# RWKV pair scores: copy on ACT and select on GpSimd in place of a masked copy on VectorE, with three DMAs of the inverse issued by GpSimd

## The chip, the cores and the metric

One NeuronCore of a Trainium2 chip runs the kernel. The metric is the device time of one execution in microseconds (us), as the median of several runs. Engines are named as the profile names them: PE is TensorE, PEld its weight loads, DVE is VectorE, ACT is ScalarE, POOL is GpSimd, SP is SyncE. Each takes its instructions strictly in the order in which they stand in its queue, so an instruction that waits holds up everything behind it on the same engine. DMAs are issued by instructions that stand in the queue of SP, ACT or POOL.

## The reference

A trunk of two layers over 256 tokens of width 1024. A layer normalises x, projects it for four mixers (stick-breaking attention, RWKV-7, MoBA, HGRN2), gates and sums their outputs, projects again, and runs a SwiGLU FFN. The change lies in the RWKV-7 mixer, which the reference computes token by token:

```
def step(state, inp):
    r_t, w_t, k_t, v_t, a_t, b_t = inp
    sa = jnp.einsum('bhvk,bhk->bhv', state, a_t)
    state = (state * w_t[:, :, None, :] + sa[..., None] * b_t[:, :, None, :]
             + v_t[..., None] * k_t[:, :, None, :])
    return state, jnp.einsum('bhvk,bhk->bhv', state, r_t)
```

The kernel computes it in two chunks of 128 tokens. For each chunk it needs, for each of 4 heads, two masked 128x128 score matrices of b against a and r (LB), the same of k (LK), and the inverse of a triangular matrix made from LB.

## The kernel before, in words

The kernel keeps x in SBUF, streams all weights from HBM as 128x1024 float32 tiles, and splits each into a high part (a cast on ACT, L128) and a low part (a subtraction on DVE, L129), so that each product is made of three matmuls (`mm3`, recorded at L80 like all matmuls). Four split weights stand in SBUF at a time. Matmul results of projections lie in the PSUM tiles `pa` (3 buffers), those of the RWKV stream in `p1` (2), those of the other three mixers in `p2` and `p3`.

`drive` interleaves two generators ("streams") with projection units: one stream is the RWKV mixer, the other runs the remaining three mixers. Each `yield` names a delay, counted on a running estimate of PE's time, after which the stream gets its next turn. The order in which instructions stand on each engine is then set by a scheduler from the order of the code and its own estimates; it sees the engine of each instruction.

In `rwkv`, for each chunk c, `pair_scores` makes the scores of four heads in two PSUM tiles. Before the change POOL fills the SBUF tile `dst` (128 x 4 x 256, of the pool `b1`) with zeros ahead of time (L536), and DVE copies the scores through the mask `armask` (`copy_predicated`, L542), once for each PSUM tile. `armask` is i<t in its first 128 columns and i<=t in its second. `pair_scores` is called four times per layer: for LB of chunk 0 and 1, then for LK of chunk 0 and 1.

The inverse goes through DRAM to change its layout: `send(c)` writes LB of chunk c to `flat` (L548, two DMAs of 256 KB); L564 reads the 64 diagonal 16x16 blocks back as `xb`, once both have landed; DVE inverts them in three levels (L570 to L594) into `yb`; L599 writes `yb` to `tri`; L602 reads it back as `cb`; L606 spreads it. Before the change all five DMAs stand in ACT's queue.

Around this stand, on ACT: the copies of stick-breaking attention's transposed weights `c<-p` (L938), which PE needs for the product with v; and, in `hgrn_proj`, `use_n` (L810, L811) which with L812 on DVE empties the two `pa` tiles of a projection. The next projection unit (a gate unit) needs the first of these buffers.

Of the kernel before, what the change touches and what calls it, by code (L numbers as in the profile page):

```python
# [15 lines left out]
OP = mybir.AluOpType  # L16
# [30 lines left out]
def trunk(ctx, tc, x, w_t, w_n, w_br, w_out, w_gu, w_dn, par, lora, rows, gains, consts, masks, out):  # L47
    nc = tc.nc
# [8 lines left out]
    def sb(tag, width, dt=F32):  # L57
        return mx.tile([128, width], dt, name=tag, tag=tag, bufs=NB[tag])

    def ps(tag):  # L60
        return psum.tile([128, 512], F32, name=tag, tag=tag, bufs=NB[tag])

    def g2d(t, a):
        return t.rearrange("p (a t) -> p a t", a=a)
# [4 lines left out]
    def over(t, n):  # L69
        return t[:, None, :].to_broadcast([128, n, t.shape[-1]])  # L70
# [3 lines left out]
    def mm(o, l, r, start=True, stop=True):  # L74
        n = 1
        for d in r.shape[1:]:
            n *= d
        m = l.shape[-1]
        pe[0] += max(m / 1.2, n / 2.4) if r.dtype == F32R else max(m / 0.6, n / 0.6)
        nc.tensor.matmul(o, l, r, start=start, stop=stop)  # L80
# [105 lines left out]
    for c in range(2):  # L186
        s = slice(c * 512, (c + 1) * 512)
# [7 lines left out]
    for i in range(20):  # L195
        nc.tensor.matmul(warm[:, 0:256], flat1[:, 0:128], flat1[:, 0:256], start=True, stop=True)
        if i in (8, 12):
            c = (i - 8) // 4
# [15 lines left out]
    yb = one.tile([64, 16, 16], F32, name="yb")  # L214
    armask = mk[:, 0:256]
# [220 lines left out]
    def head_sums(q, tag):  # L436
        p = ps(tag)
        for t in range(2):
            for hp in range(2):
                mm_cols(p[:, t * 4 + hp * 2:t * 4 + hp * 2 + 2], q[:, hp, t * 128:(t + 1) * 128], blk2)  # L440
        return p
# [4 lines left out]
    def hrow(a):  # L446
        return slice((a % 2) * 64, (a % 2) * 64 + 64)
# [17 lines left out]
    def rwkv(m, l, yT):  # L465
# [38 lines left out]
        for hp in range(2):  # L504
            s = pp[:, P_KK + hp:P_KK + hp + 1]
# [3 lines left out]
        p = head_sums(sq, "p1")  # L509
# [8 lines left out]
        p = ps("p1")  # L518
# [14 lines left out]

        def pair_scores(src, dst, c):
            p = [ps("p1"), ps("p1")]
            nc.gpsimd.memset(dst, 0.0)  # L536
            for a in range(4):
                hp = a // 2
                mm(p[a % 2][:, hp * 256:(hp + 1) * 256], src[hrow(a), hp, c * 128:(c + 1) * 128],
                   AR[hrow(a), 2 * hp + c].rearrange("p u t -> p (u t)"))  # L540
            for u in range(2):
                nc.vector.copy_predicated(dst[:, u::2], over(armask, 2), g2d(p[u], 2))  # L542

        flat = dram.tile([8, 128 * 129], F32, name="flat")
        tri = dram.tile([64, 256], F32, name="tri")

        def send(c):
            nc.scalar.dma_start(flat[4 * c:4 * c + 4, 0:128 * 128].rearrange("m (s t) -> s m t", s=128),  # L548
                                LB[c][:, :, 0:128])

        for c in range(2):
            LB.append(g2d(sb("b1", 1024), 4))
            pair_scores(bn, LB[c], c)
            yield 1600
            send(c)
# [10 lines left out]
        for c in range(2):  # L566
            LK.append(g2d(sb("b1", 1024), 4))
            pair_scores(kh, LK[c], c)
            yield 3200
# [26 lines left out]
            product(t4, blk(yb, 0, 0), blk(xb, 0, 1))  # L596
            product(blk(yb, 0, 1), t4, blk(yb, 1, 1))
        yield 4000
        nc.scalar.dma_start(tri.rearrange("p (s t) -> p s t", s=16), yb)  # L599
        yield 2500  # L600
        cb = sb("h1", 256)[:, 0:128].rearrange("p (m t) -> p m t", m=8)
        nc.scalar.dma_start(cb, bass.AP(tensor=tri.tensor, offset=tri.offset, ap=[[16, 128], [2048, 8], [1, 16]]))  # L602
# [16 lines left out]
        for c in range(2):  # L619
            z5 = z[c].rearrange("p a (b u h) -> p a b u h", u=2, h=16)  # L620
            p = ps("p1")
# [4 lines left out]
        for c in range(2):  # L626
            p = ps("p1")
# [12 lines left out]
        p = [ps("p1"), ps("p1")]  # L640
# [6 lines left out]
        p = [ps("p1"), ps("p1")]  # L647
# [11 lines left out]
        for c in range(2):  # L659
            z6.append(g2d(sb("h1", 256), 4))  # L660
            p = ps("p1")
# [4 lines left out]
        for c in range(2):  # L666
            zs.append(g2d(sb("h1", 256), 4))
            p = ps("p1")
# [5 lines left out]
        for c in range(2):  # L674
            p = ps("p1")
# [6 lines left out]
        if l:  # L682
            p = ps("p1")
# [11 lines left out]
        p = ps("p1")  # L695
# [6 lines left out]
        p = ps("p1")  # L702
# [10 lines left out]
        p = head_sums(rx, "p1")  # L713
# [7 lines left out]
        p = ps("p1")  # L721
# [8 lines left out]
        for c in range(2):  # L730
            p = ps("p1")
# [9 lines left out]
            p = ps("p1")  # L741
# [3 lines left out]
            u = sb("h1", 256)  # L745
            nc.scalar.copy(u, p[:, 0:256])
            yield 1000
            if c == 0:
                p = ps("p1")
# [7 lines left out]
                for hp in range(2):  # L757
                    for e in range(2):
                        s = hrow(e)
                        nc.vector.tensor_scalar(st[s, hp, s], p[s, hp * 64:(hp + 1) * 64], fac[s, hp:hp + 1],  # L760
                                                None, op0=OP.mult)
            p = ps("p1")
# [350 lines left out]
    def rwkv_s(m, l, yT):  # L1113
        yield from rwkv(m, l, yT)
# [181 lines left out]
```

## Time and profile before

| | us |
|---|---|
| median of 3 runs | 928.75 |
| lowest, highest | 926.98, 929.4 |
| the profiled execution: time | 930.03 |
| the profiled execution: span | 928.2 |
| PE busy in the span | 910.3 (98%) |
| DVE busy | 651.4 (70%) |
| ACT busy | 475.5 (51%) |
| POOL busy | 83.8 (9%) |

Times in the rows are counted from the start of the span. The two layers lie 452.6 us apart at the place of the change (a wait of PE that ends at 113.89 us in layer 0 ends at 566.43 us in layer 1). The granted clock is a share of TensorE's full 2.4 GHz: 0.50 is its lower level, 1.2 GHz.

### The profile page before, as it was taken

To read this page: it belongs to the slowest core of one execution; us is meant where nothing else is said; L and a number is where in the kernel's file an instruction comes from. 1 tells how busy PE (TensorE), PEld (TensorE's weight loads), DVE (VectorE), ACT (ScalarE), POOL (GpSimd) and SP (SyncE) were. 2 spreads that over 40 slices of the span, in tenths; PEclk is the share of its full clock that TensorE was granted. 3 is DMA by queue.
4 is the path that set the end of the run, shared out by engine and by line. 5 is a ranking of instruction groups with operands and counts; after the bars stand their busy time and mean duration, and the time that the engine had idled before them with its cause. 6 is when DMAs were issued, how large, how long until landed. Compare 5 with 4: busy or idle time off the path is not lost.

```text
span 928.2 us, 14996 instructions
## 1 busy us (share of the span) xinstructions
PE 910.3 (98%) x5902; PEld 761.5 (82%) x5902; DVE 651.4 (70%) x957; ACT 475.5 (51%) x726; POOL 83.8 (9%) x94
## 2 busy tenths in 40 slices
PE   8999899999999999999999998999999999999996
PEld 5999678778888888888889986767787888888885
DVE  5668877786766666677567778768678566666665
ACT  5564385445535545456445645644455345555453
POOL 3001100323000000000000201023130000000000
PEclk9999999999999999999999999999999999999999
DMA  8654454345864556568435444533368356666551
GB/s 302 204 159 137 130 175 136 114 147 166 256 220 134 183 183 184 182 206 272 155 114 161 159 140 127 186 103 115 119 208 264 114 181 204 185 182 201 181 181 46
DMA packets 50424, 158.11 MB, mean 170 GB/s; under 512 B 9393, under 2 KB 11953, under 8 KB 50354
## 3 DMA queue, kind: packets, MB, share of 16 engines
q1 hardware_dynamic: 43632, 155.19, 52.4%
q10 hardware_dynamic: 6722, 1.97, 0.9%
q8 instruction: 46, 0.75, 0.3%
q14 instruction: 24, 0.20, 0.1%
HBM read 154.91 MB, written 2.23 MB: 169 GB/s over the span
## 4 chain that ended last, share of the span: by engine, by line
PE 80%; DVE 10%; DMA 4%; issue 2%; ACT 2%; POOL 0%; SPq 0%; ACTq 0%; POOLq 0%; DVEq 0%
PE pa L80 56%; PE p L80 23%; DVE lo L129 2%; PE p L89 1%; PE pa L89 1%; DMA h<-flat 1%; DMA xr<-in_x_dram 1%; DVE b L542 1%; DMA flat<-b 1%; DVE xy L591 1%; DMA raw<-in_w_n_dram 1%; DMA lora<-in_lora_dram 1%; DMA raw<-in_w_gu_dram 1%; DVE b L867 1%; DVE b L965 1%
## 5 line engine op out<-in xcount | busy, mean ns | idle before, releaser
L129 DVE TENSOR_TENSOR lo<-raw,hi 128x1024 fp32r<-128x1024 f32 x268 | 331.0, 1240 | 153.6 <-ACT hi L128 150.6
L128 ACT CAST hi<-raw 128x1024 fp32r<-128x1024 f32 x268 | 279.2, 1048 | 225.5 <-PE pa L80 107.4
L80 PE MATMUL pa<-h,hi 128*128 128x256 f32 (+1 forms) x1280 | 277.9, 339 | 0.0
L80 PEld LDWEIGHTS pa<-h,hi 128*128 128x128 f32 x1280 | 215.9, 190 | 24.6 <-issue 2.0
L80 PE MATMUL pa<-hi,h 128*128 128x512 f32 x576 | 194.1, 402 | 4.6 <-DVE p L812 4.6
L80 PE MATMUL pa<-h,lo 128*128 128x256 f32 x960 | 179.9, 283 | 0.0
L80 PEld LDWEIGHTS pa<-h,lo 128*128 128x128 f32 x960 | 148.6, 191 | 7.0 <-issue 0.7
L80 PEld LDWEIGHTS pa<-hi,h 128*128 128x128 f32 x576 | 109.0, 189 | 31.5 <-DVE p L812 5.5
L80 PE MATMUL pa<-lo,h 128*128 128x512 f32 x288 | 113.6, 394 | 0.0
L80 PE MATMUL p<-hi,c 128*128 128x512 f32 (+1 forms) x352 | 113.4, 394 | 0.0
L80 PEld LDWEIGHTS p<-hi,c 128*128 128x128 f32 x352 | 66.1, 189 | 15.2 <-DVE c L129 0.6
L80 PE MATMUL p<-lo,c 128*128 128x512 f32 (+1 forms) x176 | 69.2, 393 | 0.0
L80 PEld LDWEIGHTS pa<-lo,h 128*128 128x128 f32 x288 | 54.5, 189 | 9.9
L263 POOL TENSOR_TENSOR rs<-rs,half 128x1 f32<-128x1 f32 x10 | 6.0, 597 | 471.6 <-DVE rs L262 471.6
L80 PE MATMUL pa<-hi,y 128*128 128x512 f32 x128 | 44.0, 399 | 0.1
L80 PE MATMUL p<-hi,b 128*128 128x512 f32 x128 | 41.4, 396 | 0.2 <-DVE b L129 0.2
L80 PEld LDWEIGHTS p<-lo,c 128*128 128x128 f32 x176 | 33.1, 188 | 6.8
L1033 POOL TENSOR_TENSOR p<-p,gt 128x512 f32<-128x512 f32 x16 | 30.9, 1953 | 39.4 <-DVE gt L1031 31.8
L340 DVE TENSOR_TENSOR gt<-gt,pa 128x256 f32<-128x256 f32 x80 | 33.2, 414 | 0.0
L128 ACT CAST c<-xy 128x512 fp32r<-128x512 f32 x20 | 12.4, 620 | 39.2 <-DVE xy L1136 39.2
L339 ACT COPY gt<-pa 128x256 f32<-128x256 f32 x80 | 29.3, 366 | 0.0
L80 PEld LDWEIGHTS pa<-hi,y 128*128 128x128 f32 x128 | 24.0, 188 | 6.3 <-issue 0.7
(276 smaller groups left out, 943.4 us busy)
## 6 DMA issues: line engine op xcount, KB each, us to landing
raw<-in_w_gu_dram SPq DMA_DIRECT2D x88, 512.0 KB, 3.9
raw<-in_w_n_dram SPq DMA_DIRECT2D x80, 512.0 KB, 3.6
raw<-in_w_dn_dram SPq DMA_DIRECT2D x44, 512.0 KB, 3.5
raw<-in_w_t_dram SPq DMA_DIRECT2D x40, 512.0 KB, 3.5
raw<-in_w_br_dram SPq DMA_DIRECT2D x16, 512.0 KB, 4.0
raw<-in_w_out_dram SPq DMA_DIRECT2D x16, 512.0 KB, 4.4
b<-in_gains_dram SPq DMA_DIRECT2D x4, 512.0 KB, 5.5
flat<-b ACTq DMA_DIRECT2D x4, 256.0 KB, 3.2
```

What stands on the lines that cost most here:

```text
L80: nc.tensor.matmul(o, l, r, start=start, stop=stop)
L89: nc.tensor.transpose(o, i, ident)
L128: a = nc.scalar.copy(dst[0], src)
L129: return a, (eng or nc.vector).tensor_tensor(dst[1], src, dst[0], op=OP.subtract)
L263: nc.gpsimd.tensor_tensor(dst, dst, half[:, :dst.shape[-1]], op=OP.pow)
L339: nc.scalar.copy(dst, p[:, 256:512])
L340: nc.vector.tensor_tensor(dst, dst, p[:, 0:256], op=OP.add)
L542: nc.vector.copy_predicated(dst[:, u::2], over(armask, 2), g2d(p[u], 2))
L591: nc.vector.tensor_tensor(pr[:, b, i], l4[:, b, i, None].to_broadcast(bc), r.to_broadcast(bc), op=OP.mult)
L867: nc.vector.tensor_tensor(qv, qv, t4[s, :, :, 0:1].to_broadcast([64, 2, 2 * nb, hb]), op=OP.mult)
L965: nc.vector.tensor_tensor_scan(kb, kb, reset[t][:, ::-1], 1.0, op0=OP.mult, op1=OP.add)
L1033: e.tensor_tensor(mg[f, t], mg[f, t], g, op=OP.add)
```

## The change

`pair_scores` no longer fills `dst` with zeros and no longer copies through the mask. ACT copies the whole of each PSUM tile to `dst`, and then POOL zeroes the masked part with two `affine_select` instructions, each over 4 heads x 128 columns, in place. The two `flat` DMAs and the `tri` DMA are issued by POOL in place of ACT. The two reads back (`xb`, `cb`) stay on ACT.

```diff
         def pair_scores(src, dst, c):
             p = [ps("p1"), ps("p1")]
-            nc.gpsimd.memset(dst, 0.0)
             for a in range(4):
                 hp = a // 2
                 mm(p[a % 2][:, hp * 256:(hp + 1) * 256], src[hrow(a), hp, c * 128:(c + 1) * 128],
                    AR[hrow(a), 2 * hp + c].rearrange("p u t -> p (u t)"))
             for u in range(2):
-                nc.vector.copy_predicated(dst[:, u::2], over(armask, 2), g2d(p[u], 2))
+                nc.scalar.copy(dst[:, u::2], g2d(p[u], 2))
+            for u in range(2):
+                v = dst[:, :, u * 128:(u + 1) * 128]
+                nc.gpsimd.affine_select(v, v, [[0, 4], [1, 128]], OP.is_ge, 0.0, base=u - 1, channel_multiplier=-1)
...
         def send(c):
-            nc.scalar.dma_start(flat[4 * c:4 * c + 4, 0:128 * 128].rearrange("m (s t) -> s m t", s=128),
+            nc.gpsimd.dma_start(flat[4 * c:4 * c + 4, 0:128 * 128].rearrange("m (s t) -> s m t", s=128),
                                 LB[c][:, :, 0:128])
...
         yield 4000
-        nc.scalar.dma_start(tri.rearrange("p (s t) -> p s t", s=16), yb)
+        nc.gpsimd.dma_start(tri.rearrange("p (s t) -> p s t", s=16), yb)
```

Line numbers behind this place are two higher after the change. PE's order is the same in both kernels. The orders of ACT, POOL and DVE differ, in both layers alike.

ACT before, from the last cast ahead of the `flat` DMAs to the copies L938 (`flat` is written from LB, h is `xb`, c the attention weights, p_954 and the like are PSUM tiles):

```order
L960 ACTIVATE b_944<-b_933 128x1024
L961 ACTIVATE b_933<-b_933 128x1024
L128 CAST hi<-raw 128x1024
L548 DMA flat<-b_953 128x4x128
L548 DMA flat<-b_1000 128x4x128
L796 COPY p<-pa 128x512
L128 CAST hi<-raw 128x1024
L564 DMA h_1120<-flat 64x16x16
L128 CAST hi<-raw 128x1024 x2
L938 COPY c_1096<-p_1091 128x512
L938 COPY c_1103<-p_1098 128x512
```

ACT after, the same stretch:

```order
L962 ACTIVATE b_944<-b_933 128x1024
L541 COPY b_953<-p_954 128x2x256
L963 ACTIVATE b_933<-b_933 128x1024
L541 COPY b_953<-p_955 128x2x256
L128 CAST hi<-raw 128x1024
L541 COPY b_1001<-p_1002 128x2x256
L541 COPY b_1001<-p_1003 128x2x256
L128 CAST hi<-raw 128x1024
L798 COPY p<-pa 128x512
L566 DMA h_1122<-flat 64x16x16
L128 CAST hi<-raw 128x1024 x2
L940 COPY c_1098<-p_1093 128x512
```

The two `flat` DMAs are gone from ACT and four score copies have come in; the read of `flat` (L564, now L566) still stands ahead of two casts and the attention copies.

ACT before, at the end of the inverse (tri is written from `yb`, h_1372 is `cb`, p<-pa is `use_n`):

```order
L128 CAST hi<-raw 128x1024 x3
L599 DMA tri<-yb 64x256
L810 COPY p<-pa 128x256
L811 ACTIVATE p<-pa 128x256
L602 DMA h_1372<-tri 128x8x16
L810 COPY p<-pa 128x256
L811 ACTIVATE p<-pa 128x256
```

ACT after, the same stretch:

```order
L128 CAST hi<-raw 128x1024 x2
L604 DMA h_1376<-tri 128x8x16
L812 COPY p<-pa 128x256
L813 ACTIVATE p<-pa 128x256
L812 COPY p<-pa 128x256
L813 ACTIVATE p<-pa 128x256
```

The write of `tri` is gone from ACT, and the read of `tri` has moved from between the two pairs of `use_n` to ahead of both.

POOL after, the whole stretch (before, four `L536 MEMSET` stand here and the two products p<-p,cn):

```order
L969 MEMSET b_933 128x4
L544 AFFINE_SELECT b_953<-b_953 128x4x128 x2
L550 DMA flat<-b_953 128x4x128
L544 AFFINE_SELECT b_1001<-b_1001 128x4x128 x2
L550 DMA flat<-b_1001 128x4x128
L984 TENSOR_TENSOR p<-p,cn 128x512 x2
L544 AFFINE_SELECT b_1124<-b_1124 128x4x128 x2
L544 AFFINE_SELECT b_1181<-b_1181 128x4x128 x2
L601 DMA tri<-yb 64x256
L815 TENSOR_TENSOR p<-p,rws 128x256 x2
```

The selects and the DMAs of LB now alternate on one engine, and the write of `tri` stands behind the selects of LK.

## Rows read from the trace of the kernel before

**Rows 1.** Page, part 1: busy time, share of the span and instructions by engine.

```profile
PE 910.3 (98%) x5902; PEld 761.5 (82%) x5902; DVE 651.4 (70%) x957; ACT 475.5 (51%) x726; POOL 83.8 (9%) x94
```

**Rows 2.** Waits of PE, the longest: us in total, times, longest us.

```profile
PE pa L80 <- DVE p L812: 4.6, 2, 2.3
```

**Rows 3.** Timeline of PE: start us, us, what, idle before; one row per layer.

```profile
113.89 0.50 PE L80 MATMUL pa<-hi,h 128*128 128x512 f32 x1 [2.33 <-DVE p L812]
...
566.43 0.50 PE L80 MATMUL pa<-hi,h 128*128 128x512 f32 x1 [2.30 <-DVE p L812]
```

**Rows 4.** Chain that ended last, layer 0, 83 to 119 us: start us, us, what.

```profile
88.81 3.23 DMA flat<-b
...
92.12 3.92 DMA h<-flat
...
111.49 0.68 DVE yb L594
...
112.19 0.49 ACTq L599
...
112.72 0.07 ACT p L810
```

**Rows 5.** Timeline of ACT, layer 0, 81 to 116 us.

```profile
81.17 1.06 ACT L960 ACTIVATE b<-b 128x1024 f32<-128x1024 f32 x1 [0.54 <-DVE b L929]
82.26 1.06 ACT L961 ACTIVATE b<-b 128x1024 f32<-128x1024 f32 x1
...
89.23 0.59 ACT L796 COPY p<-pa 128x512 f32<-128x512 f32 x1 [4.97 <-DVE b L542]
...
94.79 1.07 ACT L938 COPY c<-p 128x512 f32<-128x512 f32 x2
...
115.33 0.38 ACTq L602 DMA_DIRECT2D h<-tri  x1
```

**Rows 6.** Timeline of PE, layer 0: scores of LB and LK, attention times v.

```profile
84.51 1.89 PE L80 MATMUL p<-b,c 64*128 64x256 f32 x8
...
95.26 1.14 PE L80 MATMUL p<-b,c 64*128 64x256 f32 x8
96.33 1.14 PE L80 MATMUL p<-c,p 128*64 128x128 f32 x16
```

**Rows 7.** Timeline of DVE, layer 0, 100 to 114 us.

```profile
100.47 1.33 DVE L542 COPY_PREDICATED b<-mk,p 128x512 f32<-128x512 uint8 x2
101.70 0.99 DVE L981 TENSOR_TENSOR c<-c,cn 128x512 f32<-128x512 f32 x1
...
103.82 0.68 DVE L981 TENSOR_TENSOR c<-c,cn 128x512 f32<-128x512 f32 x1
...
112.08 1.21 DVE L129 TENSOR_TENSOR lo<-raw,hi 128x1024 fp32r<-128x1024 f32 x1
```

**Rows 8.** Groups of POOL by form: busy us, mean ns of one, idle before.

```profile
L1033 POOL TENSOR_TENSOR p<-p,gt 128x512 f32<-128x512 f32 x16 | 30.9, 1953 | 39.4 <-DVE gt L1031 31.8 <-DVE bs L715 7.6
...
L982 POOL TENSOR_TENSOR p<-p,cn 128x512 f32<-128x512 f32 x4 | 4.3, 1096 | 32.9 <-DVE c L980 32.9
...
L263 POOL TENSOR_TENSOR var<-var,half 128x4 f32<-128x4 f32 x4 | 4.1, 1016 | 28.6 <-DVE var L262 28.6
...
L238 POOL MEMSET reset<- 128x512 f32 x2 | 1.0, 520 | 0.0
```

**Rows 9.** DMA issues: KB each, median us from issue to landing.

```profile
tri<-yb ACTq DMA_DIRECT2D x2, 64.0 KB, 3.1
```

**Rows 10.** Stretches around the wait: busy (x) by engine, PEclk, DMA share, GB/s.

```profile
114.00:116.00 2.00, 2.00 (x7) 1.63 (x8) 1.36 (x4) 0.25 (x1) 0.65 (x1) 0.73 0.88 262
116.00:118.00 2.00, 2.00 (x6) 1.52 (x6) 1.04 (x2) 1.98 (x4) 1.06 (x2) 0.50 0.73 188
118.00:120.00 2.00, 2.00 (x10) 1.61 (x9) 2.00 (x4) 1.99 (x8) 0.57 (x1) 0.92 0.12 23
...
566.00:568.00 2.00, 1.57 (x7) 1.31 (x8) 1.90 (x5) 0.00 (x0) 0.73 (x1) 1.00 0.91 292
```

## The prediction

> **What bounds the kernel now.** I read the page's busy times first. PE is busy 98% of the span [rows 1], its order of instructions is the same after the change, and no matmul is added or removed. So the change can only move the few microseconds in which PE stands still. Next I read who PE waits for: by far the longest entry is the wait for L812, 4.6 us in two waits [rows 2], one in each layer, 2.33 and 2.30 us [rows 3]. Then I followed the chain that ends in the first of these waits backwards [rows 4]. PE wants a `pa` buffer; L812 on DVE empties it, but needs L810 and L811 of ACT; these stand in ACT's queue behind the issue of the `tri` DMA (112.19), which waits for the last step of the inverse on DVE (111.49 + 0.68 = 112.17). The inverse starts when `xb` lands (92.12 + 3.92 = 96.04), and that starts when the second `flat` DMA lands (88.81 + 3.23 = 92.04). So the end of PE's wait, 113.89, is set by a chain that begins with the scores of LB, and the change touches nearly every link. The clock is the last thing to read: behind the wait in layer 0 the granted clock is 0.73, 0.50, 0.92 in three stretches of 2 us, so PE was on its lower level for part of it and lost 2 x (0.27 + 0.50 + 0.08) = 1.7 us; behind the wait in layer 1 it is 1.00 at once [rows 10]. So all that can be won by removing these waits is 4.6 + 1.7 = 6.3 us, 0.7% of the time.
>
> **The change part by part.** I work in layer 0's times; layer 1 has the same waits within 0.03 us [rows 3].
>
> *VectorE loses the masked copies.* Four pairs of L542 per layer go. Two of the pairs lie inside the inverse, one at 100.47 and one eight microseconds later; each holds DVE for 101.70 - 100.47 = 1.23 us until the next instruction starts, say 1.25 [rows 7]. The changed order also puts one weight split more behind the inverse that stood ahead of its last step; a split takes 1.21 us [rows 7], of which neighbours overlap a little: about 1.1. From `xb` to the finished `yb` took 112.17 - 96.04 = 16.1 us; 2 x 1.25 + 1.1 = 3.6 come off, which leaves 12.5 us. This is the gain.
>
> *ACT gets the copies.* A copy of 128x512 from PSUM (L796) takes 0.59 us [rows 5]. The first stands behind L960, the second behind L961, so LB of chunk 0 is copied at 81.17 + 1.06 + 0.59 + 1.06 + 0.59 = 84.5. PE wanted the buffers for the scores of chunk 1 at 84.51 and then took 1.89 us where the eight rows of LK take 1.14 [rows 6], since it waited for L542. That wait of 0.8 us goes, and chunk 1 is copied by 84.5 + 1.1 + 2 x 0.59 = 86.8. Eight copies are 4.7 us of ACT per layer. What hides them: ACT stood idle 4.97 us ahead of L796 [rows 5], in front of the `flat` DMAs that leave it.
>
> *POOL gets the selects.* No `affine_select` is in the trace. Its bounds are the nearest rows of POOL at 128x512: 0.52 us for a fill that reads nothing, 1.10 for a product of two tiles at this very place, 1.95 for a product beside a busy DVE [rows 8]. I take t = 1.1, since a select reads and writes and stands where L982 stands. The fills that go were idle time on POOL, so they give nothing back.
>
> *POOL issues `flat` and `tri`.* No DMA of POOL is in the trace either. I write g for what such a DMA takes more than one of ACT, and let the issue hold up POOL as long. From below it is 0, if it flies like ACT's. From above I take one whole further flight, 3.1 us [rows 9]. I take g = 1.0, since a POOL instruction with almost no data, 128x4, takes 1.02 [rows 8], and the issue is at least such an instruction. The Trainium skill, "DMA: Bandwidth & Descriptors", section "Specifications", states about 1 us to the first byte for a DMA of GpSimd, whose descriptors are written by software, against 0.6 us for one of sync or scalar; by that, an estimate from the page, g would be 0.4 and the sum below +0.7 us per layer in place of +2.5. No row here shows it.
>
> *The sum.* Selects of chunk 0, its DMA's issue, selects of chunk 1, its DMA: the second `flat` lands at 84.5 + 2t + g + 2t + g + 3.23 = 94.1, where it landed at 92.04. `xb` lands at 94.1 + 0.05 + 3.92 = 98.1, `yb` is ready at 98.1 + 12.5 = 110.6, which is 1.6 us earlier than now. `tri` lands at 110.6 + g + 3.1 = 114.7. But the read of `tri`, L604, now stands ahead of both pairs of `use_n`, while before only the short issue of the write stood ahead of the first. So ACT's first copy comes at 114.7 + 0.5 = 115.2, where it came at 112.72 [rows 4]. From that copy to PE's restart it took 113.89 - 112.72 = 1.2 us: PE restarts at 116.4, 2.5 us later than now. In short, the shift per layer is 4t + 3g - 4.9 us. The round trip of `tri` has taken the place of what DVE saved.
>
> *A new wait on the way.* ACT waits at L566 for `flat`, and behind it stand two casts and the attention copies L940. Before, L938 was done 94.79 + 1.07 - 92.04 = 3.8 us after `flat` landed [rows 5], and PE used it at 96.33 without a wait [rows 6]. After, it is done at 97.9, while PE, with its 0.8 us saved, comes at 95.5: a wait of 2.4 us, which leaves PE 1.6 us later than now. It does not add to the shift at 116.4, which is later still; it only splits PE's standstill in two: PE came to the `pa` wait at 113.89 - 2.33 = 111.56, comes now at 113.2, and waits 3.2 us there. The casts behind L566 fill split weights ahead of the one that PE works on (four stand at a time), which covers a shift of 2 us; were that cover gone, PE would wait for them as long as ACT is late. LK has time: PE needs it tens of microseconds later. The read `cb` is issued at 114.7 against 115.33 now [rows 5], so the steps behind it are not late.
>
> Two layers give +5.0 us. For the clock I take one more drop like that of layer 0 (1.7 us), since the last waits become longer than 2.3 us in both layers; none more to three more are possible, 0 to 5.1 us. Forecast: +6.7 us.
>
> **The rivals.**
>
> *POOL's part is cheap: no change.* If a DMA of POOL flies nearly like one of ACT (g from 0 to 0.4) and t is 1.1, the shift is -0.5 to +0.7 per layer, -1 to +1.4 us in all: 928 to 930. For it: the data and their destinations are the same. Against it: all three POOL DMAs are in series with the chain, and so are the four selects.
>
> *Faster.* The mechanism is the relief of DVE at L594: `yb` comes so early that even with the read of `tri` in front ACT's copies come before 112.72. This decides from 4t + 3g below 4.9. With a select at the fill's price, 0.52, and g = 0, the selects of chunk 1 start when its copies are done, `flat` lands at 86.8 + 1.04 + 3.23 = 91.1, and PE restarts at 91.1 + 0.05 + 3.92 + 12.5 + 3.1 + 0.5 + 1.2 = 112.4, 1.5 us earlier; with layer 0's clock drop gone as well that is -3.0 - 1.7 = -4.7 us, 924. It needs both unknowns at their lower ends.
>
> *POOL is held up by DVE: much slower.* L981 on DVE takes 0.99 us while POOL's L982 runs and 0.68 once it is over [rows 7], and POOL's product of 128x512 costs 1.95 in place of 1.10 where DVE is busy [rows 8]; DVE runs scans, products and splits all through the selects of LB. With t = 1.95 and g = 3.1 the shift is 7.8 + 9.3 - 4.9 = 12.2 per layer, 24 us, with the clock 29 us: 958. With t = 1.5 and g = 2 it is 7.1 per layer, with three clock drops 19 us: 948. The Trainium skill, "SBUF — State Buffer", section "Who interferes with whom", states that a VectorE instruction with two SBUF inputs contends with a GpSimd instruction that reads SBUF, and that one blocks for the other's whole length; the rows of L981 agree in direction (0.31 us), not in that a whole instruction is lost.
>
> *The change does not do what it says:* POOL's DMAs are handled exactly like ACT's. That is the cheap rival's end, g = 0.
>
> **How the numbers follow.** The profiled execution took 930.03 us, span 928.2, and lies 1.3 above the median; the difference I forecast is the same for both, so I give it on the median: 928.75 + 6.7 = 935.45, say 935.5. About 0.3%, 2.8 us, is what a measurement of this kernel can tell from no change. Chances: the forecast, 931.5 to 943, 0.56; much slower, 0.18; POOL cheap, 0.20; faster, 0.06. The range leaves out the faster case and the upper part of the much slower one: 928.5 to 949. Of the cheap case a little ends above +2.8 us with a clock drop: slower 0.77, same 0.17, faster 0.06.
>
> **What the changed profile would show.** PE waits in each layer at two places: at the attention product p<-c,p for ACT's L940 (some 2.4 us) and at pa<-hi,h for L814 (some 3.2 us). ACT is idle ahead of L128 behind L566, and ahead of L812, both put down to a DMA. POOL's selects come in pairs of about 2.2 us; the second `flat` lands near 94.1; `yb` is ready near 110.6 and `tri` lands near 114.7. It would be wrong if `flat` lands before 92 and `tri` before 112, or if PE's wait for L814 is gone; and too low if a select takes 2 us or a POOL DMA twice the time of ACT's.

## The result, and the profile after

The changed kernel takes 932.39 us (median of 8 runs, 930.62 to 933.02) beside 928.68 us for the kernel before on the same chip (8 runs, 924.40 to 929.42). The ratio is 1.0051, with a 95% interval from 1.0034 to 1.0069: +4.7 us (3.2 to 6.4; the medians lie 3.7 apart), where +6.7 was forecast. The profiled execution took 933.02 us, the longest of the eight; its span is 931.3 (928.2 before). In the kernel after, the lines of the RWKV mixer stand two numbers higher from L543 on: L814 is the old L812, L604 the old L602.

The page's busy times; POOL has 13 us more than before, VectorE 3 less [rows 1]:

```profile
PE 911.1 (98%) x5902; PEld 762.6 (82%) x5902; DVE 648.2 (70%) x941; ACT 482.4 (52%) x742; POOL 97.1 (10%) x108
```

The waits of PE (us in total, times, longest); the first answers to [rows 2], the second is new:

```profile
PE pa L80 <- DVE p L814: 5.9, 2, 2.9
...
PE p L80 <- ACT c L940: 0.8, 2, 0.5
```

The timeline of PE where it stood still: the attention product and the two waits for `pa`, which answer to [rows 3], and a last small one in layer 0:

```profile
96.08 1.58 PE L80 MATMUL p<-c,p 128*64 128x128 f32 x16 [0.37 <-ACT c L940]
114.55 0.79 PE L80 MATMUL pa<-hi,h 128*128 128x512 f32 x1 [2.93 <-DVE p L814]
128.00 0.50 PE L80 MATMUL pa<-hi,y 128*128 128x512 f32 x1 [0.27 <-ACT gt L1013]
...
568.59 0.79 PE L80 MATMUL pa<-hi,h 128*128 128x512 f32 x1 [2.92 <-DVE p L814]
```

PE goes on 0.66 us later than before in layer 0 (113.89) and 2.16 us later in layer 1 (566.43), of which about 1.1 were there when that layer began.

The timeline of POOL in layer 0, its new work:

```profile
84.25 2.40 POOL L544 TENSOR_SCALAR_AFFINE_SELECT b<-b 128x512 f32<-128x512 f32 x2 [0.39 <-ACT b L541]
86.60 0.97 POOL L550 DMA_DIRECT2D flat<-b  x1
87.59 1.23 POOL L544 TENSOR_SCALAR_AFFINE_SELECT b<-b 128x512 f32<-128x512 f32 x2
88.76 0.77 POOL L550 DMA_DIRECT2D flat<-b  x1
...
101.47 2.12 POOL L544 TENSOR_SCALAR_AFFINE_SELECT b<-b 128x512 f32<-128x512 f32 x2
...
110.91 0.58 POOL L601 DMA_DIRECT2D tri<-yb  x1 [5.29 <-DVE yb L596]
```

The timeline of ACT there: the read of `flat` (it marks its landing), the read of `tri` ahead of the copies, and the softmax, which comes late:

```profile
92.79 0.66 ACTq L566 DMA_DIRECT2D h<-flat  x1
...
112.90 0.44 ACTq L604 DMA_DIRECT2D h<-tri  x1
113.39 0.37 ACT L812 COPY p<-pa 128x256 f32<-128x256 f32 x1 [5.62 <-DMA tri<-yb]
...
120.25 1.28 ACT L996 ACT_TABLE_LOAD   x1 [4.72 <-DVE mxs L993]
```

The timeline of VectorE: the inverse begins at 95.77 and ends with L596 at 110.61; between them stand the products beside POOL's work, behind them the wait for `cb`:

```profile
95.77 0.16 DVE L572 COPY yb<-h 64x8 f32<-64x8 f32 x1
...
99.36 2.70 DVE L983 TENSOR_TENSOR c<-c,cn 128x512 f32<-128x512 f32 x2
101.99 1.12 DVE L985 TENSOR_TENSOR c<-c,p 128x512 f32<-128x512 f32 x1
...
104.66 1.08 DVE L593 TENSOR_TENSOR xy<-h,yb 64x64 f32<-64x64 f32 x2
...
109.93 0.68 DVE L596 TENSOR_REDUCE yb<-xy 64x64 f32<-64x512 f32 x1
...
114.08 0.42 DVE L814 TENSOR_TENSOR p<-p,pa 128x256 f32<-128x256 f32 x1 [1.20 <-ACT p L813]
...
118.48 0.69 DVE L608 TENSOR_TENSOR xy<-h,mk 128x512 f32<-128x512 f32 x1 [3.31 <-DMA h<-tri]
```

The page's DMA issues (KB each, median us from issue to landing); the second answers to [rows 9]:

```profile
h<-flat ACTq DMA_DIRECT2D x2, 64.0 KB, 2.7
tri<-yb POOLq DMA_DIRECT2D x2, 64.0 KB, 2.0
h<-tri ACTq DMA_DIRECT2D x2, 64.0 KB, 5.4
```

Stretches behind the two waits (us, PE busy, granted clock, DMA share, GB/s), for [rows 10]:

```profile
114.00:116.00 2.00, 1.45 (x4) 0.62 0.99 387
116.00:118.00 2.00, 2.00 (x6) 0.52 0.41 65
...
568.00:570.00 2.00, 1.42 (x3) 0.62 0.98 356
570.00:572.00 2.00, 2.00 (x6) 0.53 0.46 87
```

Layer 0 loses 2 x (0.38 + 0.48) = 1.7 us to the lower level, as before; layer 1, which had 1.00 before, now loses 1.7 as well. With the shifts of about 1.1 us in each layer that makes some 3.8 us, of which 0.7 is gone again by the end of the span (3.1 us longer).

### The profile page after: what moved, and what is told of

It is laid out like the page before. It is cut to its first block, busy times and chain, and to the rows that moved or that the text cites. A ratio compares the mean times of both kernels' runs of the same rounds, so it can differ in the third digit from the quotient of the medians.

```text
span 931.3 us, 15007 instructions
## 1 busy us (share of the span) xinstructions
PE 911.1 (98%) x5902; PEld 762.6 (82%) x5902; DVE 648.2 (70%) x941; ACT 482.4 (52%) x742; POOL 97.1 (10%) x108
## 4 chain that ended last, share of the span: by engine, by line
PE 87%; DVE 5%; issue 3%; ACT 3%; DMA 1%; POOL 1%; ACTq 0%; POOLq 0%; DVEq 0%
PE pa L80 61%; PE p L80 23%; PE pa L89 1%; PE p L89 1%; ACT hi L128 1%; DVE lo L129 1%; POOL b L544 1%; DVE b L869 1%; PE pa L196 0%; DMA flat<-b 0%; DMA raw<-in_w_t_dram 0%; DMA tri<-yb 0%; PE p L199 0%; DVE xr L411 0%; ACT c L996 0%
## 5 line engine op out<-in xcount | busy, mean ns | idle before, releaser
L80 PE MATMUL p<-hi,c 128*128 128x512 f32 (+1 forms) x352 | 113.5, 394 | 0.0
```

## The experiments

Two kernels fix the ends: the one before and the one after. The others do one part of the change alone, or the whole change with one thing moved. "Wait" is PE's wait at `pa` in layer 0 and layer 1. Each ratio is to the kernel before on the same chip, where its median was 927.88 to 928.97 us; so for kernels that ran on different chips the ratios are the fairer comparison.

| kernel | median us | ratio to before (95%) | waits, us |
|---|---|---|---|
| after | 932.39 | 1.0051 (1.0034-1.0069) | 2.93, 2.92 |
| 1 DMAs alone | 926.02 | 0.9987 (0.9972-1.0001) | 1.32, 1.38 |
| 2 copies and selects alone | 933.69 | 1.0079 (1.0058-1.0099) | 5.18, 5.05 |
| 3 after, read of `tri` on POOL | 931.69 | 1.0053 (1.0035-1.0071) | 2.55, 1.64 |
| 4 after, selects twice | 942.61 | 1.0176 (1.0153-1.0198) | 4.03, 3.36 |
| 5 LB alone | 931.68 | 1.0035 (1.0018-1.0053) | 2.93, 2.91 |
| 6 LK alone | 932.65 | 1.0048 (1.0034-1.0062) | 3.39, 3.46 |
| 7 write of `tri` alone | 929.03 | 1.0010 (0.9995-1.0025) | 2.10, 2.08 |
| 8 DMAs and read of `tri` | 927.06 | 1.0001 (0.9983-1.0019) | 1.30, 1.25 |
| 9 LB alone, fills on VectorE | 929.05 | 1.0023 (1.0008-1.0038) | 2.01, 2.34 |
| 10 writes of `flat` alone | 926.06 | 0.9988 (0.9971-1.0005) | 1.56, 1.84 |
| 11 DMAs, `pa` copied out | 931.99 | 1.0062 (1.0038-1.0085) | none here |
| 12 after, read of `tri` on SP | 927.46 | 0.9984 (0.9972-0.9996) | 1.76, 1.90 |

### 1. The DMAs alone

```
 pair_scores as in the kernel before
-nc.scalar.dma_start(flat[...], LB[c][...])
+nc.gpsimd.dma_start(flat[...], LB[c][...])
-nc.scalar.dma_start(tri..., yb)
+nc.gpsimd.dma_start(tri..., yb)
```

> The kernel before with only the two DMA kinds moved: `flat` and `tri` are issued by GpSimd, the masked copies stay on VectorE. ACT then has its first two pairs of copies for `pa` ahead of the read of `tri`, since the write no longer stands in its queue. Theory 1 (the loss comes from the order on ACT, where the read of `tri` stands ahead of both pairs; a POOL DMA itself costs under 1 us more and its flight no more than one of ACT): `flat` lands 0.7 later, the read of `xb` is 0 to 0.9 shorter, `yb` ready between 112.0 and 113.0, PE restarts between 113.5 and 114.6 against 113.9 before, so the time is between 928 and 931, within 0.3% of before. Rival 1 (DMAs of POOL are slow in themselves, about 1 us each in series): three in a row give +2 to +3 us per layer, 933 to 935. Rival 2 (the selects and not the DMAs cost): 928.7, nothing at all.

Measured: 926.02 us, at the lower edge of "no change" (the interval just takes in 1), and below what any theory gave. ACT's first pair stands ahead of everything that waits for `yb`; its timeline:

```profile
107.84 0.37 ACT L810 COPY p<-pa 128x256 f32<-128x256 f32 x1 [0.30 <-PE pa L80]
...
114.51 0.41 ACTq L602 DMA_DIRECT2D h<-tri  x1
```

PE's timeline in the same run:

```profile
112.72 0.50 PE L80 MATMUL pa<-hi,h 128*128 128x512 f32 x1 [1.32 <-DVE p L812]
```

The inverse starts at 95.2 in place of 96.07 and PE goes on 1.17 us earlier; the clock stays at 1.00 in both layers. So DMAs of POOL, three in series per layer, are no loss here, and rival 1 falls: what the change costs lies in the copies and selects, or in what they do to the order.

### 2. The copies and selects alone

```
 copies on ACT, selects on GpSimd, as in the kernel after
-nc.gpsimd.dma_start(flat[...], ...)   and   nc.gpsimd.dma_start(tri..., yb)
+nc.scalar.dma_start(flat[...], ...)   and   nc.scalar.dma_start(tri..., yb)
```

> The kernel after with the two DMA kinds given back to ACT; copies on ACT and selects on GpSimd stay. In ACT's queue both the write and the read of `tri` stand ahead of the two pairs of copies. Theory 1: `flat` is issued without POOL's 0.8 to 1.0 us and lands some 0.5 to 1 us earlier than in the kernel after, but `tri` takes 3.1 us from ACT instead of 2.0 to 2.6, so PE's restart stays within 0.6 us of the kernel after: 931 to 933.5. Rival 1 (slow POOL DMAs are the loss): back to 928 to 929.5. Rival 2 (selects beside VectorE are the loss): 932 to 933, not told from theory 1 by this run alone.

Measured: 933.69, the same as the kernel after or a little more; rival 1 falls again. In this execution PE's first matmuls ran faster (four of 1x512 in 2.21 us, in the others in 3.78), so all rows stand 2.7 us earlier. ACT's timeline:

```profile
108.58 0.50 ACTq L601 DMA_DIRECT2D tri<-yb  x1
109.19 1.04 ACT L128 CAST hi<-raw 128x1024 fp32r<-128x1024 f32 x1 [8.11 <-DVE yb L596]
110.55 0.38 ACTq L604 DMA_DIRECT2D h<-tri  x1
111.05 1.04 ACT L128 CAST hi<-raw 128x1024 fp32r<-128x1024 f32 x1 [0.82 <-DMA tri<-yb]
112.00 0.37 ACT L812 COPY p<-pa 128x256 f32<-128x256 f32 x1
```

Write, cast, read, cast, and only then the copy: PE waits 5.18 us, 2.2 more than in the kernel after, and goes on at 113.74 + 2.7 = 116.4. My 0.6 us for that was wrong, since I had counted the DMAs and not the two casts that stand behind them. Behind these waits of 5 us the clock costs 3.4 us in each layer, twice what it costs in the kernel after. `tri` took 1.97 us from ACT here, not the 3.1 that I had put to ACT's queue.

### 3. The kernel after, with the read of `tri` on GpSimd

```
-nc.scalar.dma_start(cb, ...tri...)
+nc.gpsimd.dma_start(cb, ...tri...)
```

> The kernel after with one more DMA moved: the read of `tri` is issued by GpSimd too, so ACT's pairs of copies for `pa` stand behind no DMA. Theory 1: ACT's copies run as soon as `pa` is there, and L814 on VectorE is then held only by its own place behind `yb` (110.6) and two weight splits (to 112.9); PE restarts near 113.3 in layer 0 instead of 114.55, and its wait falls from 2.9 to some 1.7 us; with both layers 1.2 x 2 = 2.5 us come back, and the clock drop of 1.7 in layer 1 may go as well: 928 to 930.5. Against it a little: the scores' mask product L608 waits for `cb` and holds the second L814 behind it. Rival 1 (DMAs of POOL are slow): one more such DMA makes it slower, 933 to 935. Rival 2 (the inverse slowed by POOL's work sets the end): `yb` is not earlier, so no change, 932.4.

Measured: 931.69, by its ratio not told apart from the kernel after (1.0053 and 1.0051); 928 to 930.5 was expected. PE's timeline in layer 0:

```profile
113.62 0.50 PE L80 MATMUL pa<-hi,h 128*128 128x512 f32 x1 [2.55 <-DVE p L814]
...
122.34 0.50 PE L80 MATMUL pa<-lo,h 128*128 128x512 f32 x1 [1.40 <-DVE lo L129]
```

VectorE's timeline:

```profile
118.33 0.69 DVE L608 TENSOR_TENSOR xy<-h,mk 128x512 f32<-128x512 f32 x1 [4.10 <-DMA h<-tri]
```

The first half went as theory 1 says: PE goes on 0.93 us earlier than in the kernel after (1.97 in layer 1), and no clock drop is left. But L608 stands on VectorE ahead of the softmax's L992, the second L814 and the next split; it waits for `cb`, which is as late as before, and PE then waits 1.40 us per layer for that split and 0.5 for what follows. What I had called "a little against it" took nearly all of the gain. So to free ACT's copies of the read is not enough while `cb` itself lands late.

### 4. The kernel after, with each select issued twice

```
-for u in range(2):
+for u in (0, 1, 0, 1):
     nc.gpsimd.affine_select(...)
```

> The kernel after with every select issued twice (the second changes nothing), so that its price t doubles, by the trace of the kernel after from 0.92 to 1.84 us on average. By the formula of the prediction the restart of PE moves by 4t, that is +3.7 us per layer, +7.4 us in all, and with a longer wait of PE perhaps one clock drop more: 939 to 942. Rival 2 (selects also slow VectorE's work beside them): more than 4t, over 942. Rival 3 (only the clock drop of layer 1 is the loss, the chain has slack): under 935.

Measured: 942.61, 10.2 us over the kernel after, more than 4t. The selects ahead of the second `flat` take 4.55 + 3.39 us in place of 2.40 + 1.23: 4.3 us later, that is 4t with t = 1.08. The inverse takes 16.5 us, 1.6 longer. PE's waits (us in total, times, longest):

```profile
PE p L80 <- ACT c L940: 8.1, 2, 4.1
PE pa L80 <- DVE p L814: 7.4, 2, 4.0
```

So the selects do stand in series, and they slow VectorE on top; the wait at the attention product that I had put at 2.4 us for the change exists, at a larger shift.

### 5 and 6. One half of the scores each

```
+if src is kh:                       # run 5; "src is bn" in run 6
+    nc.gpsimd.memset(dst, 0.0), then copy_predicated on VectorE as before
 else: copies on ACT and selects on GpSimd, as after; DMAs as after
```

> Half of the change: the scores of LB (which feed `flat`) are copied by ACT and selected on GpSimd, those of LK stay masked copies on VectorE; all DMAs as in the kernel after. In this order both pairs of copies for `pa` stand ahead of the read of `tri` on ACT, and on VectorE the mask product that waits for `cb` stands behind both pairs. Theory A (what costs is the end of the chain: the read of `tri` ahead of the copies on ACT, and the late `cb` ahead of the second pair on VectorE; both come with LK's copies on ACT): `flat` lands at 92.8 as in the kernel after, the inverse keeps its two masked copies and ends near 111.5 to 112.0, PE restarts near 113.2 to 113.8 with a wait of 1.5 to 2 us; the time is 927 to 930, no slower than before. Rival B (what costs is the selects in series with `flat`): 930.5 to 932.5, most of the loss.

> The other half: LB's masked copies stay on VectorE, only LK is copied by ACT and selected on GpSimd; all DMAs as in the kernel after. The read of `tri` stands ahead of both pairs of copies on ACT, with one cast of a weight between them, and the mask product that waits for `cb` ahead of the second pair on VectorE. The inverse loses its two masked copies (2.5 us) and runs beside the selects. Theory A: `yb` near 110, `tri` lands near 112.5, PE restarts between 114 and 115.5 with a wait near 3 us, a clock drop in both layers: 930.5 to 934, most of the loss. Rival B: `flat` lands as in the run with the DMAs alone and VectorE is freer, so it is faster than that run: 923.5 to 926. For the inverse: if the selects slow it as in the kernel after, it takes 14.5 to 15 us, if not, 12.5.

Measured: LB alone 931.68, LK alone 932.65; by the ratios +3.2 and +4.5 us, where both together make +4.7. For LK theory A holds: `yb` is ready at 109.37, `tri` lands at 111.66, and ACT has a cast ahead of the copies once more:

```profile
112.19 1.04 ACT L128 CAST hi<-raw 128x1024 fp32r<-128x1024 f32 x1 [7.23 <-DMA tri<-yb]
113.14 0.36 ACT L818 COPY p<-pa 128x256 f32<-128x256 f32 x1
```

PE goes on at 114.87, and both layers lose 1.7 us to the clock. The inverse takes 14.1 us here, so LK's selects slow it without those of LB. For LB theory A failed, by an edit of mine: the fills that LK's masked copies need now stood in POOL's queue between the first `flat` and the selects of chunk 1. POOL's timeline:

```profile
87.56 1.87 POOL L537 MEMSET b<- 128x1024 f32 x2
...
90.56 0.78 POOL L556 DMA_DIRECT2D flat<-b  x1
```

`flat` is 1.8 us late by that, and `yb` (113.5) and PE (115.01) with it.

### 9. LB alone, without the fills on GpSimd

```
-nc.gpsimd.memset(dst, 0.0)
+nc.vector.memset(dst, 0.0)
```

> The run with LB alone once more, with one difference: the two fills that LK's masked copies need are made on VectorE, which is idle there, and no longer stand on POOL between the first `flat` DMA and the selects of chunk 1 (they took 1.87 us of the chain in that run). In ACT's queue the read of `tri` stands between the two pairs, as in the kernel before. Theory C (POOL's order put the fills in series with `flat`, and the selects themselves cost only what the masked copies cost there): the second `flat` is issued near 88.8 and lands near 92.3, `yb` near 111.3 to 112.0, PE restarts at 113.0 to 113.8, no clock drop or one: 926 to 929. Rival B (selects of LB cost in any case): 930 to 932.

Measured: 929.05, 2.6 less than run 5 and 1.1 more than the kernel before, at the upper end of theory C; by the ratios the gain over run 5 is 1.1 us and their intervals overlap, so the trace has to carry this step. `flat` is issued where it is in the kernel after and PE goes on at 112.8 (110.84, and 2.0 for a faster start as in run 2), 2.2 us ahead of run 5. What is left over the kernel with the DMAs alone, 3 us, stands in the profile as one clock drop of 1.7 in layer 0 and a wait of 1.31 for a split in layer 1. So LB's half costs about 3 us over run 1 and LK's half 6.6, as much as both together (6.4; by the ratios 3.3, 5.7 and 5.9); the halves do not add up. LK's half alone brings the order in which the read of `tri` stands ahead of both pairs.

### 7 and 10. Which DMA gives run 1 its time

```
 kernel before, with only the write of tri (run 7), only the writes of flat (run 10) on nc.gpsimd
```

> The kernel before with one DMA moved: only the write of `tri` is issued by GpSimd, `flat` stays on ACT. Theory A: what the run with both DMA kinds gained (PE's wait 1.3 us in place of 2.3, no clock drop) comes from the write of `tri` leaving ACT's queue: ACT's first pair for `pa` no longer waits for `yb`, so PE's wait falls to 1.3 to 2.0 us; the time is 925 to 927.5. Rival: it came from `flat` on GpSimd (an earlier `xb`): then 928 to 929, as before.

> The kernel before with one DMA kind moved: only the two `flat` writes are issued by GpSimd, the write and the read of `tri` stay on ACT. In the runs with `flat` on GpSimd the read of `xb` took at most 2.7 to 3.6 us, with `flat` on ACT 3.8 to 3.95. Theory D (what the run with both DMA kinds gained came from an earlier `xb`): the inverse starts near 95.2 in place of 96.05, `yb` is ready near 111.3, PE restarts 0.7 to 1 us earlier than before, near 113.0; 926 to 928. Rival (it came from both DMAs together, since the write of `tri` holds ACT's copies until `yb` is ready): PE restarts where it did, 113.9; 928 to 929.

Measured: 929.03 and 926.06. My theory A fell: `tri` alone gives no time, although ACT's first pair is done at 108.57, since L812 has its place on VectorE behind `yb` and a split, and starts at 113.10 where it started at 113.41. `flat` alone gives as much as run 1 (0.9988 and 0.9987; neither interval leaves out 1). VectorE's timeline of run 10:

```profile
94.06 1.23 DVE L129 TENSOR_TENSOR lo<-raw,hi 128x1024 fp32r<-128x1024 f32 x1 [3.85 <-ACT hi L128]
95.21 0.16 DVE L570 COPY yb<-h 64x8 f32<-64x8 f32 x1
```

The inverse starts 0.86 us earlier, since the read of `xb` is shorter (2.7 us against 4.0), and PE goes on 0.93 us earlier; without a clock drop. SyncE's timeline has a likely reason. In the kernel before, a weight load of 512 KB is issued just ahead of that read (92.12):

```profile
92.05 0.33 SPq L133 DMA_DIRECT2D raw<-in_w_n_dram  x1
```

In run 10 it is issued 1.96 us ahead of the read (92.20):

```profile
90.24 0.33 SPq L133 DMA_DIRECT2D raw<-in_w_n_dram  x1
```

The load comes earlier because ACT, without the writes of `flat` to wait for, does a cast at 87.91 that stood at 89.71, and so the split behind the cast is done earlier; in both kernels the load starts as that split ends (90.21 and 92.03). Run 7, whose `flat` stayed on ACT, has the load at 92.02, the read at 92.01 and 4.0 us once more. No run moved the load alone.

### 8 and 11. Two ways to get more from run 1

```
 run 8: read of tri on nc.gpsimd too
 run 11, use_n:
+nc.scalar.copy(f, p[:, 256:512])
-nc.vector.tensor_tensor(gs[:, t], gs[:, t], p[:, 256:512], op=OP.mult)
+nc.vector.tensor_tensor(gs[:, t], gs[:, t], f, op=OP.mult)
```

> The run with the DMAs alone on GpSimd, and the read of `tri` moved there too: ACT has no DMA ahead of either pair of copies, and on VectorE the product that waits for `cb` stands behind both pairs and a split. Theory A: PE's first wait is set by VectorE (`yb`, one weight split, then L812), so it stays at 1.3 us; no gain, and none lost since nothing but that product waits for `cb`: 925 to 927. Rival (a late `cb` always costs, as in the run with `cb` on GpSimd): 927.5 to 930.

> The run with the DMAs alone on GpSimd, and one more edit: ACT copies the second half of `pa` out to SBUF (one more copy of 128x256, 0.37 us), and VectorE multiplies from that copy. So `pa` is free without VectorE, whose product stands behind `yb` and a weight split. The same results are computed. Theory A (PE waits 1.3 us per layer for VectorE alone, since ACT's pair is done at 108.5): the wait at the first `pa` goes, PE goes on at 111.4; 2 x 1.3 us less than that run, 922.5 to 925, if no later wait takes it back; the second `pa` is free only behind the read of `tri`, near 115.5 to 116.5, which could cost up to 1 us per layer. Rival (another wait of the same length follows at once): 925.5 to 927.5.

Measured: 927.06 and 931.99. In run 8 the wait at `pa` stays 1.3 as theory A says, and a wait of 1.36 us per layer for a split comes behind it, since `cb` lands late (3.92 us of waiting at L606); the time lies between both theories. In run 11 the wait at `pa` is gone, as theory A says, and the rival is right about the time. PE's timeline:

```profile
119.97 0.51 PE L80 MATMUL pa<-hi,h 128*128 128x512 f32 x1 [1.77 <-ACT hi L128]
121.94 0.50 PE L80 MATMUL pa<-lo,h 128*128 128x512 f32 x1 [1.46 <-DVE lo L129]
```

The scheduler, with one copy more on ACT, put the next cast behind the softmax (118.89 in place of 115.51), and PE waits for that cast and its split, 3.2 us in place of 1.3, with one clock drop of 1.7 in layer 0.

### 12. The kernel after, with the read of `tri` on SyncE

```
-nc.scalar.dma_start(cb, ...tri...)
+nc.sync.dma_start(cb, ...tri...)
```

> The kernel after, with the read of `tri` issued by SyncE: it stands there between two weight loads, so ACT has no DMA ahead of its pairs for `pa`, and two of the three weight loads that flew at the same time as `cb` in the kernel after (DMA engines busy 0.98 to 1.00 of the time from 114 to 116, `cb` 5.4 us) come behind it. The selects, the inverse and `yb` (110.6) stay as they are. Theory E (what is left of the loss is the read ahead of ACT's pairs, plus the late `cb` that holds VectorE): PE restarts at 113.2 to 113.7, `cb` lands by 116.5 and no longer holds the second pair, PE does not wait for a weight split behind it, no clock drop or one: 926.5 to 929.5. Rival F (the slowed inverse and the selects in series are the loss): 931 to 933 as the kernel after. Rival G (the weight loads held behind the read are late in their turn): PE waits for casts some microseconds on, 930 to 934.

Measured: 927.46, 4.9 us less than the kernel after (6.2 by the ratios), as theory E says, and a little less than the kernel before. PE's timeline in layer 0:

```profile
112.94 0.50 PE L80 MATMUL pa<-hi,h 128*128 128x512 f32 x1 [1.76 <-DVE p L814]
```

SyncE's timeline (DMA issues):

```profile
111.45 0.33 SPq L133 DMA_DIRECT2D raw<-in_w_n_dram  x1
112.64 0.38 SPq L604 DMA_DIRECT2D h<-tri  x1
113.51 10.17 SPq L133 DMA_DIRECT2D raw<-in_w_n_dram  x3
```

VectorE's timeline:

```profile
116.23 0.69 DVE L608 TENSOR_TENSOR xy<-h,mk 128x512 f32<-128x512 f32 x1 [2.68 <-DMA h<-tri]
```

`cb` takes 3.6 us in place of 5.4 and lands 2.2 us earlier; the clock is at 1.00 behind both waits; PE does not wait for weights that were held behind the read. The selects and the slowed inverse are all still there (`yb` at 110.29, against 110.61). So what made the kernel after slower than the one before is the place of one DMA, the read of `tri`: ahead of ACT's copies, and amid the weight loads. Run 3 shows that the first alone is not the loss; the second alone was not tried.

## Why the prediction was right

*What bounds the kernel, and the mechanism.* Right. PE moves mainly where it waits for L814; ACT's L812 comes 0.5 us behind the landing of `tri`, and 1.16 us later PE goes on (0.5 and 1.2 in the prediction). Run 12 takes that read away from ACT, and out of the burst of weight loads, and the loss is gone.

*The forecast.* +4.7 against +6.7, inside its case. Per layer the step was +2.5; it measured +0.66 in layer 0 (+1.13 by 128 us) and about +1.0 in layer 1. The clock term, one drop more of 1.7 us, came as forecast. So the chain's 5.0 us came out at some 2.1 in the profile, less than half; the total is nearer than that because the clock's 1.7 was right.

*Copies on ACT and t.* Right for the first copies (84.2 and 86.8, in the sum 84.5 and 86.8). A select takes 1.2 us beside a busy VectorE and 0.6 us beside an idle one; I took 1.1 for all. *g* for `flat`: POOL is held 0.97 and 0.77 us, near the 1.0. That was luck in part: the 1.02 us of [rows 8] was one row of its kind, and a fill of 128x4 on POOL took 0.10 us in the same trace (L967). Together `flat` landed at 92.79, 1.3 us ahead of the sum, most of it from the second pair of selects.

*From `flat` to the inverse.* Mis-sized: the read of `xb` took 2.7 us, not 3.92; the old one flew just behind a weight load (runs 7 and 10), the new one 2.86 us behind. The inverse began at 95.77, behind a split, and not at 98.1.

*The inverse.* The term that failed most: 12.5 us in the sum, 110.61 - 95.77 = 14.84 measured. The masked copies did go, but beside POOL's product and selects L983 took 2.70 us for two (0.99 + 0.68 in [rows 7]), L985 1.12 in place of 0.68, and a pair of 64x64 products 1.08 in place of 0.44, 2.1 us in all. In run 5, without selects beside the inverse, these rows have about their old lengths and the inverse takes 16.1 us with the masked copies. I had used the row of L981 for the rival "held up by DVE" alone, and not turned it round: POOL holds up VectorE too. The loss of 2.3 us against the sum and the 2.3 us of the earlier start cancel, so `yb` at 110.6 is right by luck. The Trainium skill, "SBUF — State Buffer", section "Who interferes with whom", has this pair of instructions contending; L985's 0.44 us more again is part of a select, not the whole of one.

*`tri`.* Mis-sized by 1.8 us: from `yb` to the landing 1.0 + 3.1 in the sum, 112.90 - 110.61 = 2.3 measured, 0.3 to the issue and 2.0 of flight. This is why PE went on at 114.55 and not at 116.4. The 3.1 came from a flight issued 0.6 us behind a weight load (111.59 and 112.19); the nearest load ahead of the new one was issued 2.7 us earlier (108.25 and 110.91). By the price of the Trainium skill's "DMA: Bandwidth & Descriptors", section "Specifications", an estimate which I had set beside the sum, the shift was +0.7 per layer. That this lies near what came is luck; the flights do not show its reason, since `tri` from POOL was shorter than from ACT, not longer.

*The wait at the attention product.* There, at 0.37 us and not 2.4, since `flat` was earlier.

*"The steps behind `cb` are not late."* Wrong in effect: `cb` was issued 2.4 us earlier than before (112.90), took 5.4 us where it had taken 2.7, and was in use at 118.48, hardly ahead of the old one at 118.68. L608, which waits for it, now stands on VectorE ahead of the softmax, the second L814 and the next split, and holds them. It put 0.27 us on PE at 128.00, and runs 3 and 8 show what it holds when the first wait shrinks.

*The rivals.* "Faster" needed both prices at their lower ends; the second pair of selects came near (0.6 us), the first pair and the issues of the DMAs did not. "Much slower" was right that POOL and VectorE slow each other, but selects beside a busy VectorE took 1.2 us and not 1.95, and the greater loss was on VectorE. "Cheap" was right about the DMAs (run 1).

## What to carry to other kernels

Before work is moved to an idle engine, write out what then stands ahead of the next waiting engine's releaser in each queue: here the DMAs of POOL cost nothing (run 1), the selects no more than the masked copies, as far as the times can tell (run 12 and run 1 take 0.9984 and 0.9987 of the time before), and one DMA read that slid ahead of two small copies and flew amid weight loads cost all of it. Price contention both ways when work goes to POOL beside VectorE. When a DMA that a chain waits for has been read off a trace, look at what was issued just ahead of it before its time is put into a sum; here two such times fell by 1.1 to 1.3 us when a weight load no longer stood beside them. Try such a DMA ahead of the burst of weight loads, on the queue that issues the burst if need be; in run 12 this paid.

## What the runs showed of the hardware

- The read of `xb` (64 KB, always issued by ACT) took 3.7 to 4.0 us (medians of the page) in the three kernels whose `flat` was written from ACT's own queue, and 2.6 to 3.3 us in the eleven in which POOL issued those writes. How closely it followed a weight load separates them nearly as well: in the first three the two were issued within 1.2 us of each other, in ten of the eleven the read came 1.7 us or more behind the load; the last, run 9, has 1.1 to 1.2 us and took 3.3. No run parted queue and load.
- The write of `tri` took 3.1 to 3.9 us (medians of the page) when it was issued 0.6 to 0.9 us behind a weight load (before, runs 1, 7, 8, 10, 11) and 1.9 to 2.2 us in the others, 1.9 us or more behind one, from POOL or ACT alike (run 2: 1.9 from ACT).
- Two-input products of VectorE stretch beside POOL: in the kernel after, a 64x64 pair of the inverse took 1.08 us beside selects, where it took 0.44 before; a pair of reductions, with one input, took 0.33 in both. Splits beside the selects of LB took 1.58 to 1.65 us in place of 1.22.
- The granted clock fell behind every wait at `pa` of 2.9 us or more (after, runs 2, 4, 5, 6) and stayed at 1.00 behind those of 1.3 to 1.9 us (runs 1, 3, 8, 10, 12). Between 2.0 and 2.6 us it did either: it fell behind 2.33 (before), 2.08 (run 7) and 2.01 (run 9), and not behind 2.30, 2.10, 2.34 and 2.55 (before, runs 7, 9, 3). A drop cost 1.7 us, in run 2 3.4. The waits of runs 1, 10 and 12 are 0.4 to 1.0 us shorter than those before, and their profiles lack the drop of 1.7 us as well.
- The kernel before itself lies between 924.2 and 930.0 over all its runs. Two executions show one thing that is worth some 2 us: PE's first four matmuls of 1x512 took 2.21 and 2.27 us in the profiled runs 2 and 9 and 3.77 to 3.78 in the others, and what follows stands 2.7 and 2.0 us earlier there. The one profile of the kernel before has the longer form, so that its faster executions are of this kind is not shown.
